# Entry of the second feed-forward block: two joins of squares by accumulating DMAs, two weights and tiles of the first operands sooner, differences in two steps

## The chip, the cores and the metric

The kernel runs on one core of one Trainium2 chip. The metric is the device time of one execution in microseconds (us); three runs of the kernel before took 2147.59, 2148.53 and 2149.14 us, median 2148.53. Five engines work side by side, each through its own queue in order: TensorE (PE, matmuls; PEld is its loading of weights), VectorE (DVE), ScalarE (ACT), GpSimd (POOL, here an issuer of DMAs) and SyncE (SP, an issuer of DMAs). They wait for each other through semaphores. ScalarE issues some DMAs too.

## What is computed

A decoder trunk of two layers on 1024 tokens with 1024 channels, in float32. Each layer is a mixer (a short gated convolution in the first, dilated attention in the second) and a SwiGLU feed-forward block of width 2816, each behind an RMS norm and with a residual sum:

```
def rms_norm(x, g):
    xf = x.astype(jnp.float32)
    y = xf * lax.rsqrt(jnp.mean(xf * xf, axis=-1, keepdims=True) + EPS)
    return (y * g.astype(jnp.float32)).astype(x.dtype)
...
def swiglu(h, w_gate, w_up, w_down):
    return (jax.nn.silu(h @ w_gate) * (h @ w_up)) @ w_down
...
    for i in range(DEPTH):
        h = rms_norm(x, mix_norm[i])
...
            x = x + dilated_attention_mixer(h, attn_w_qkv[j], attn_w_out[j], rel_bias)
        h = rms_norm(x, ffn_norm[i])
        x = x + swiglu(h, ffn_w_gate[i], ffn_w_up[i], ffn_w_down[i])
    return rms_norm(x, final_norm)
```

The place in question is the passage from the attention's output projection (`wo`) to the gate and up products of the second layer's feed-forward block: the residual x gets its last sums, its squares are summed over the channels, the reciprocal root is spread over all rows, and the scaled x becomes the operand of the next products.

## The kernel before

**Tiles.** The activations lie with channels on the 128 rows and tokens along them, as eight tiles `X[n]` of 128x1024. Nearly all work is done on halves of 512 tokens, one PSUM bank each. Every float32 operand is split in a high part (ScalarE, L139 for weights, L546 for activations) and a low part (VectorE, source minus high part, L140 and L547); one product then is three matmuls: high by high, high by low, low by high (L365 to L367 in `product`, L554 to L556 in `mm`).

**Strassen units.** Gate and up products are done by Strassen's seven products of 2x2 blocks. The blocks of the activations are the two halves of the channels (tiles 0 to 3, tiles 4 to 7) by the two halves of the tokens. Operand 1 is the first channels of the first token half, operand 2 the last channels of it; 6, 7, 4, 5 and 3 need the second token half or differences of the two. `unit_order` gives the order of (unit, product): n = 0 is (0, 1), then (1, 1), (0, 2), (1, 2), (2, 1), (2, 2), (3, 1), (3, 2), (0, 6), (1, 6), (0, 7), (1, 7), (0, 4), (1, 4), (0, 5), (1, 5) and so on. Each of these products is twelve matmuls of 128x512. `products` calls `start(n)` of `feed_forward` after the n-th one, and there the next preparations stand.

**Order of work.** The program is written out by hand in one order; every engine takes its instructions in that order. `ensure(upto)` has the weight splits made up to an index of the list `ops`, and `load_raw` with it the loads of raw weights that these need, through SP's queue.

**The output projection at the entry.** `by_columns` runs the last three of eight k tiles of `wo` over the first token half (j = 0), then over the second (j = 1), for n = 0 to 7. After each piece `add_to_x` sums the bank into x (L487), `added` has weights made, `each` is `Norm.chained` and squares the tile (L439), and `between` stores x to DRAM (the spill, L1286) and does the preparations of the feed-forward block. In the second pass, `between` first takes the statistics of the first token half: `Norm.stats` sums the squares over the rows with tiny matmuls (L466), takes root and reciprocal (L469, L470), makes diagonal tiles (L475), spreads them by a matmul (L482) and copies the result to `rstd` (L483). Then each step n does `step(k)`: one step of `first_half` (scale tile k of the first token half, L1107; high part L546; low part L547, one tile behind) and `gained(k)` (the second token half of tile k times its gain, L1129; from k = 4 on an accumulating DMA of POOL, L1133, makes tile k minus tile k-4 out of it).

**Sums of squares.** `chained` keeps two accumulators, `acc` for even and `odd` for odd tiles. Tiles 2 and 3 are added by accumulating DMAs of POOL (L442). From tile 4 on, in the second block (`late`), tile 4 is kept as `rest`; tiles 5 and 6 are added to it by VectorE (L454), `odd` is added to `acc` (L440) at tile 6, and at tile 7 `rest` and then the square of tile 7 are added to `acc`: five adds of VectorE. This goes for both token halves.

**The second half's operands.** After n = 2 (second block; 1 in the first) the statistics of the second token half begin, and after the next product `second_half` starts: its first stage makes operands 7 and 6; then, at n = 5, 7, 8, 10 and 12, one stage each: four differences for operand 4; its high and low parts with four multiplications by `rstd`; four differences for operand 5; parts of 5; parts of 3. VectorE does all but the high parts. The same `feed_forward` serves both blocks, with key 0 and 1.

Of the kernel before, what the change touches and what calls it, by code (L numbers as in the profile page):

```python
# [13 lines left out]
ALU = mybir.AluOpType  # L14
# [7 lines left out]
KT = D // 128  # L22
# [73 lines left out]
def trunk(ctx: ExitStack, tc: tile.TileContext, x, gains_in, cwi, ck, cwo, wqkv, wo, relb,  # L96
          wg, wu, wd, oneh, ident, out):
    nc = tc.nc
# [6 lines left out]
    def page(name, dt=F32):  # L105
        return pages.tile([128, 1024], dt, name=name, tag="page", bufs=PAGES)
# [3 lines left out]
    def half_page(name, dt=F32):  # L110
        return scope["pool"].tile([128, 512], dt, name=name, tag="half", bufs=scope["halves"])
# [4 lines left out]
    def half(h):  # L116
        return slice(h * HALF, (h + 1) * HALF)
# [42 lines left out]
    def ensure(upto):  # L160
        while op_state[0] < min(upto + 1, len(ops)):
            key = ops[op_state[0] + 1][0] if op_state[0] + 1 < len(ops) else None
            if key in sums_of:
                sums_of.pop(key)()
            made[op_state[0]] = ops[op_state[0]][1]()
            op_state[0] += 1
# [203 lines left out]
    def run(*gens):  # L370
        for _ in zip(*gens):
            pass
        for g in gens:
            for _ in g:
                pass
# [14 lines left out]
    class Norm:  # L390
# [30 lines left out]
        def add(self, k):  # L421

            hi, lo = page("h_hi", F32R), page("h_lo", F32R)
            nc.scalar.activation(hi, X[k], AF.Identity, scale=self.gain(k))
            nc.vector.scalar_tensor_tensor(lo, X[k], self.gain(k), hi, op0=ALU.mult, op1=ALU.subtract)
            self.h[k] = (hi, lo)
            self.square(k)

        def chained(self, k, c0, c1, late):


            s = slice(c0, c1)
            if self.acc is None:
                self.acc, self.rstd = page("acc"), page("rstd")
            acc = self.acc[:, s]
            if k == 1:
                self.odd = half_page("acc2")
            to = half_page("sq") if k > 1 else self.odd if k else acc
            nc.scalar.activation(to, X[k][:, s], AF.Square)  # L439
            add = lambda t: nc.vector.tensor_tensor(out=acc, in0=acc, in1=t, op=ALU.add)  # L440
            if k in (2, 3):
                nc.gpsimd.dma_start(out=(acc, self.odd)[k % 2], in_=to, accum_op=ALU.add)  # L442
            if k > 3:
                self.flush()
                self.put_off = lambda: add(to)
            if k == KT - 2:
                add(self.odd)
                self.odd = None
            if not late or k < 4:
                return  # L450
            if k == 4:
                self.rest, self.put_off = to, None
            elif k < KT - 1:
                add = lambda t: nc.vector.tensor_tensor(out=self.rest, in0=self.rest, in1=t, op=ALU.add)  # L454
            else:
                add(self.rest)
                self.rest = None
# [27 lines left out]
    def add_to_x(n, banks):  # L485
        for (c0, c1), b in banks.items():
            nc.vector.tensor_tensor(out=X[n][:, c0:c1], in0=X[n][:, c0:c1], in1=b[:, :c1 - c0], op=ALU.add)  # L487
# [608 lines left out]
    class Swiglu(Strassen):  # L1096
# [38 lines left out]
        def second_half(self):  # L1135

            tt = lambda out, a, b, op: nc.vector.tensor_tensor(out=out, in0=a, in1=b, op=op)
            rstd = self.norm.rstd[:, half(1)]
            t3, h, f = self.xd, {k: self.xg[4 + k] for k in range(4)}, self.f
            t2 = {k: X[4 + k][:, half(1)] for k in range(4)}  # L1140
            low7, low = [], None
            for k in range(4):
                tt(t3[k], t3[k], rstd, ALU.mult)
                low7.append(self.hi(7, k, t3[k]))
            for k in range(4):
                tt(t2[k], t3[k], f[k], ALU.add)
                nxt = self.hi(6, k, t2[k])
                if low:
                    low()
                low = nxt  # L1150
            low7.pop(0)()
            low()
            for lo in low7:
                lo()
            yield

            for k in range(4):
                tt(f[4 + k], f[4 + k], t2[k], ALU.subtract)
            yield
            lows = [self.hi(4, k, f[4 + k]) for k in range(4)]  # L1160
            for k in range(4):
                tt(h[k], h[k], rstd, ALU.mult)
            for lo in lows:
                lo()
            yield
            for k in range(4):
                tt(f[k], h[k], t2[k], ALU.subtract)
            yield
            lows = [self.hi(5, k, f[k]) for k in range(4)]
            for lo in lows:  # L1170
                lo()
            yield
            lows = [self.hi(3, k, h[k]) for k in range(4)]
            for lo in lows:
                lo()
            X[:] = [None] * KT
# [31 lines left out]
        def feed_forward(self, stats, last_step, after, final=None):  # L1208
            prep = []

            def start(n):
                if n == 0:
                    last_step()
                    for m in (6, 7):
                        combos[self.key, 1](m)
                    ensure(self.at(3, 1))
                if n == self.key + 1:
                    next(stats)
                    combos[self.key, 2](6)
                    ensure(self.at(0, 6))  # L1220
                elif n == self.key + 2:
                    run(stats)
                    prep.append(self.second_half())
                    next(prep[0])
                    nc.scalar.activation(scratch, eps, AF.Silu)
                    ensure(self.at(1, 6))
                elif n == 4:
                    ensure(self.at(1, 7))
                elif n in (5, 7, 8, 10, 12):
                    next(prep[0], None)  # L1230
                if n in (8, 24):
                    self.ahead = 3 if n == 8 else 2

            self.run(start)
            key = ("d", self.key)
            if final:
                final(key, self.plain, self.hid)
                return
            for n in range(KT):
                add_to_x(n, both(take(key + (n,)), self.plain, self.hid))  # L1240
                after(n)
# [22 lines left out]
    def into_ffn(i, norm):  # L1264

        sw = Swiglu(i, norm)

        pre = []
        first_op = [k for k, f in ops].index(("m", (i, 0), 1))

        def step(k):
            next(pre[0], None)
            sw.gained(k)

        def group1(key, ks, acts):
            def added(j, n):

                if j == 0 and n > 2:
                    if 3 < n < KT - 2:
                        ensure(op_state[1] + 1)  # L1280
                    ensure(first_op + n - 2)
                elif j and n in (2, 3):
                    ensure(first_op + n + 4)

            def between(j, n):
                nc.scalar.dma_start(spill[n][:, half(j)], X[n][:, half(j)])  # L1286
                if j == 0:
                    if n == 2:
                        load_raw(raw_base[i] + 3)
                    elif n == 3:  # L1290
                        if not i:
                            nc.scalar.activation(less, gains, AF.Copy, scale=-1.0)
                    elif n == 4 and last_part:
                        last_part.pop()()
                    elif n == KT - 1:
                        norm.flush()
                    return
                if n == i:
                    pre.append(norm.stats(0, HALF))
                    next(pre[0])  # L1300
                    for m in (6, 7):
                        combos[i, 0](m)
                elif n == i + 1:
                    run(pre.pop())
                    pre.append(sw.first_half())
                for k in (((), (0,), (1,), (2, 3), (4,)), ((), (), (0, 1), (2, 3), (4,)))[i][n] if n < 5 else (n,):
                    step(k)

            by_columns((key, 1), ks, acts, HALVES, lambda n, c: norm.chained(n, *c, i), between,
                       AO_WIDE if key == "ao" else 4, added=added)  # L1310

        def last_step():
            run(pre[0])
            norm.flush()

        return sw, group1, norm.stats(HALF, S), last_step
# [620 lines left out]
```

## Time and profile before

| | |
|---|---|
| runs, median (lowest to highest) | 2148.53 us (2147.59 to 2149.14) |
| profiled execution, its own time | 2150.36 us |
| its span, first to last instruction | 2148.5 us |
| mean granted TensorE clock | 0.996 |
| half clock, second entry | 1508.0 to 1514.8 us |
| second pass of the output projection | about 1480 to 1497 us |
| first gate and up products of the second block | from 1496.8 us |

How to read the lines that follow: a timeline row gives start, duration, engine, line, operation, output and input tiles, shape and count, and in brackets the idle time ahead of it with what ended it. A row of a chain gives start, duration, what. A row of a list of waits gives the engine and its line, what released it, the sum of the waits, how many, the longest. A row of a stretch gives the busy time and count of PE, PEld, DVE, ACT and POOL, then the granted clock, the DMA engines' mean busy share and GB/s. A row of DMA issues ends with the size of one and the median time from issue to landing in us; a queue's row has packets, MB and the share of sixteen DMA engines' time. Durations of instructions that follow each other on one engine overlap by some 0.1 us, so a start-to-start distance is shorter than a duration (0.60 for 0.69 on VectorE). Line numbers are those of the kernel before.

### The profile page before, as it was taken

The numbers are of one execution on the slowest core, as the hardware profiler recorded it, in microseconds if no ns is written. First come the engines' busy times: TensorE is split into PE (matmuls) and PEld (weight loads), VectorE is DVE, ScalarE is ACT, GpSimd is POOL, SyncE is SP. The second block draws the span as 40 slices with busy tenths as digits, with TensorE's granted clock in tenths as the row PEclk, the third lists the DMA queues.
The fourth block names the chain that finished last, engine by engine and source line by source line (L and its number), as shares of the span: only waits on it lengthen the run. The fifth ranks groups of instructions, "written<-read, shape, count | busy, mean of one in ns | idle before, by whom it ended". The sixth has DMA issues, their size and how long they took to land.

```text
span 2148.5 us, 30610 instructions
## 1 busy us (share of the span) xinstructions
PE 2122.4 (99%) x11158; PEld 1819.3 (85%) x11158; DVE 1721.4 (80%) x3192; ACT 1011.3 (47%) x1836; POOL 183.6 (9%) x239
## 2 busy tenths in 40 slices
PE   9999999999999999999999999999999999999998
PEld 7788888888888888878999999888788888888887
DVE  7898769988888888865777777777998888888886
ACT  7433426443444564344555555535544444456435
POOL 1000000110101000010111111111010101001000
PEclk9999999999999999999999999999999999999999
DMA  7222642223332576323333333636223332368432
GB/s 227 84 94 69 225 132 74 103 99 108 113 109 98 171 220 194 113 63 128 89 93 93 93 93 86 193 120 188 64 80 107 113 108 103 102 206 231 163 94 79
DMA packets 135055, 264.49 MB, mean 123 GB/s; under 512 B 47912, under 2 KB 59192, under 8 KB 134906
## 3 DMA queue, kind: packets, MB, share of 16 engines
q1 hardware_dynamic: 74106, 177.99, 26.0%
q0 software_dynamic: 19632, 61.46, 9.2%
q10 hardware_dynamic: 41168, 23.10, 3.5%
q8 instruction: 88, 1.44, 0.3%
q14 instruction: 61, 0.50, 0.1%
HBM read 188.88 MB, written 66.27 MB: 119 GB/s over the span
## 4 chain that ended last, share of the span: by engine, by line
PE 88%; DVE 6%; ACT 3%; issue 2%; DMA 1%; SPq 0%; ACTq 0%; DVEq 0%
PE bank L554 18%; PE bank L556 18%; PE bank L555 17%; PE bank L367 6%; PE bank L365 6%; PE bank L366 6%; PE bank L1529 5%; PE bank L646 3%; PE bank L649 3%; PE bank L648 3%; PE bank L1457 1%; PE bank L1456 1%; DVE w L140 1%; PE bank L1397 1%; PE bank L1396 1%
## 5 line engine op out<-in xcount | busy, mean ns | idle before, releaser
L554 PE MATMUL bank<-b,w 128*128 128x512 f32 x1784 | 698.7, 392 | 3.6 <-ACT part L560 2.1
L556 PE MATMUL bank<-b,w 128*128 128x512 f32 x1784 | 696.5, 390 | 4.4 <-DVE w L140 4.4
L555 PE MATMUL bank<-b,w 128*128 128x512 f32 x1784 | 696.8, 391 | 2.8 <-DVE b L547 2.2
L556 PEld LDWEIGHTS bank<-b,w 128*128 128x128 f32 x1784 | 335.8, 188 | 77.3 <-DVE w L140 7.3
L554 PEld LDWEIGHTS bank<-b,w 128*128 128x128 f32 x1784 | 335.9, 188 | 74.5 <-ACT part L560 3.3
L555 PEld LDWEIGHTS bank<-b,w 128*128 128x128 f32 x1784 | 336.1, 188 | 72.9 <-DVE b L547 3.1
L139 ACT ACTIVATE w<-combo 128x512 fp32r<-128x512 f32 (+2 forms) x464 | 233.9, 536 | 223.0 <-DVE combo L187 188.1
L140 DVE TENSOR_TENSOR w<-combo,w 128x512 fp32r<-128x512 f32 (+2 forms) x464 | 260.4, 575 | 39.0 <-ACT w L139 38.3
L560 ACT ACTIVATE part<-bank 128x512 f32<-128x512 f32 x168 | 100.2, 597 | 375.5 <-PE bank L556 373.9
L140 DVE TENSOR_TENSOR w<-raw,w 128x512 fp32r<-128x512 f32 (+2 forms) x316 | 170.5, 560 | 36.7 <-ACT w L139 36.7
L564 DVE TENSOR_TENSOR part<-part,bank 128x256 f32<-128x256 f32 (+1 forms) x348 | 158.7, 488 | 26.9 <-PE bank L556 16.2
L139 ACT ACTIVATE w<-raw 128x512 fp32r<-128x512 f32 (+2 forms) x316 | 150.5, 520 | 45.9 <-DVE w L140 11.2
L365 PE MATMUL bank<-w_hi,w 128*128 128x512 f32 (+1 forms) x320 | 119.7, 374 | 1.0 <-ACT w L139 1.0
L367 PE MATMUL bank<-w_hi,w 128*128 128x512 f32 (+1 forms) x320 | 118.0, 369 | 0.7 <-DVE w L140 0.7
L366 PE MATMUL bank<-w_lo,w 128*128 128x512 f32 (+1 forms) x320 | 117.8, 368 | 0.0
L784 DVE TENSOR_TENSOR x<-x,bank 128x512 f32<-128x512 f32 x136 | 92.8, 682 | 29.3 <-PE bank L556 29.3
L487 DVE TENSOR_TENSOR x<-x,bank 128x512 f32<-128x512 f32 (+1 forms) x104 | 66.1, 643 | 54.5 <-PE bank L367 52.7
L365 PE MATMUL bank<-h_hi,w_hi 128*128 128x512 f32 x256 | 104.5, 408 | 0.2 <-ACT w_hi L139 0.2
L187 DVE TENSOR_TENSOR combo<-raw 128x512 f32<-128x512 f32 (+1 forms) x160 | 103.2, 645 | 0.0
L367 PE MATMUL bank<-h_hi,w_lo 128*128 128x512 f32 x256 | 100.2, 391 | 0.6 <-DVE w_lo L140 0.5
L366 PE MATMUL bank<-h_lo,w_hi 128*128 128x512 f32 x256 | 99.9, 390 | 0.0
L1552 ACT ACTIVATE z<-bank 64x512 f32<-64x512 f32 x32 | 19.0, 594 | 145.3 <-PE bank L1529 145.3
(261 smaller groups left out, 3889.8 us busy)
## 6 DMA issues: line engine op xcount, KB each, us to landing
hin<-part SPq DMA_DIRECT2D x126, 256.0 KB
raw<-in_ffn_w_gate SPq DMA_DIRECT2D x44, 512.0 KB
raw<-in_ffn_w_up SPq DMA_DIRECT2D x44, 512.0 KB
part<-sum POOLq DMA_DIRECT2D x72, 256.0 KB, 2.3
raw<-in_ffn_w_down SPq DMA_DIRECT2D x48, 384.0 KB
raw<-in_conv_w_in SPq DMA_DIRECT2D x24, 512.0 KB
raw<-in_attn_w_qkv SPq DMA_DIRECT2D x24, 512.0 KB
part<-part POOLq DMA_DIRECT2D x36, 256.0 KB, 2.4
```

Source lines behind the costliest of these rows:

```text
L139: nc.scalar.activation(hi, src, AF.Copy)
L140: eng.tensor_tensor(out=lo, in0=src, in1=hi, op=ALU.subtract)
L187: eng.tensor_tensor(out=c, in0=a, in1=b, op=op)
L365: nc.tensor.matmul(b, whi[:, a], ahi[:, s], start=first, stop=False)
L366: nc.tensor.matmul(b, whi[:, a], alo[:, s], start=False, stop=False)
L367: nc.tensor.matmul(b, wlo[:, a], ahi[:, s], start=False, stop=last)
L554: nc.tensor.matmul(b, hi[:, a], bhi, start=start and k == 0, stop=False, skip_group_check=True)
L555: nc.tensor.matmul(b, hi[:, a], blo, start=False, stop=False, skip_group_check=True)
L556: nc.tensor.matmul(b, lo[:, a], bhi, start=False, stop=k == n - 1, skip_group_check=True)
L560: nc.scalar.activation(t, b, AF.Copy)
L564: nc.vector.tensor_tensor(out=t, in0=t, in1=b, op=ALU.add)
L1529: nc.tensor.matmul(view(acc[ih], off, dims), vx[:, u, 64 * a:64 * a + 128], rhs, start=first, stop=last)
```

## The change

Four edits, in `chained`, `second_half` with `feed_forward`, `added`, and `between`:

- In the second block and the second token half alone, `odd` goes into `acc` by an accumulating DMA at tile 4, and the square of tile 5 into `rest` by another at tile 5. Tile 6 is added to `acc` by VectorE, as are `rest` and tile 7: three adds.
- The four differences for operand 4 are two stages of two, and n = 9 takes a stage too. So the stages stand at n = 5, 7, 8, 9, 10 and 12: two differences, two differences, parts of 4 with the multiplications, differences for 5, parts of 5, parts of 3 (both blocks).
- In the second block the weights of products (3, 1) and (3, 2) are split at n = 1 and 2 of the second pass, before at n = 2 and 3.
- In the second block `first_half` takes two steps at each of n = 2, 3 and 4 and one at each of n = 5, 6 and 7, apart from `gained`; before it took one with each `gained`, two at n = 2 and 3, one at n = 4 to 7, and the last low part behind the loop.

```
@@ chained
+            if late and c0:
+                if k == 4:
+                    self.rest = to
+                    nc.gpsimd.dma_start(out=acc, in_=self.odd, accum_op=ALU.add)
+                    self.odd = None
+                elif k == 5:
+                    nc.gpsimd.dma_start(out=self.rest, in_=to, accum_op=ALU.add)
+                elif k > 5:
+                    self.flush()
+                    self.put_off = lambda: add(to)
+                if k == KT - 1:
+                    add(self.rest)
+                    self.rest = None
+                return
@@ second_half
             for k in range(4):
                 tt(f[4 + k], f[4 + k], t2[k], ALU.subtract)
-            yield
+                if k % 2:
+                    yield
@@ feed_forward
-                elif n in (5, 7, 8, 10, 12):
+                elif n in (5, 7, 8, 9, 10, 12):
                     next(prep[0], None)
@@ added
-                elif j and n in (2, 3):
-                    ensure(first_op + n + 4)
+                elif j and n in (2 - i, 3 - i):
+                    ensure(first_op + n + 4 + i)
@@ between
-                for k in (((), (0,), (1,), (2, 3), (4,)), ((), (), (0, 1), (2, 3), (4,)))[i][n] if n < 5 else (n,):
-                    step(k)
+                if i:
+                    for _ in range((0, 0, 2, 2, 2, 1, 1, 1)[n]):
+                        next(pre[0], None)
+                    for k in ((), (), (0, 1), (2, 3))[n] if n < 4 else (n,):
+                        sw.gained(k)
+                else:
+                    for k in ((), (0,), (1,), (2, 3))[n] if n < 4 else (n,):
+                        step(k)
```

In the changed order of the engines, PE's instructions and SP's are the same; VectorE has two adds fewer, ScalarE the same instructions in another order, POOL two DMAs more. POOL's queue in the second token half is: square 2 into `acc`, square 3 into `odd`, `odd` into `acc` (which waits for both to land), the first difference, square 5 into `rest`, the other three differences. On VectorE the add of square 6 waits for the third of these, the add of `rest` for the fifth, and the low part of the last tile of operand 2 stands behind both.

## The prediction

> **What bounds the kernel now.** I read the page first, then the list of PE's waits, then the stretch of the second entry in stretches, by engine and along the chain.
>
> ```profile
> span 2148.5 us, 30610 instructions
> PE 2122.4 (99%) x11158; PEld 1819.3 (85%) x11158; DVE 1721.4 (80%) x3192; ACT 1011.3 (47%) x1836; POOL 183.6 (9%) x239
> PE 88%; DVE 6%; ACT 3%; issue 2%; DMA 1%; SPq 0%; ACTq 0%; DVEq 0%
> ```
>
> TensorE is the bound: it idles 26 us in all. The change takes no matmul away, so it can only win PE's stalls at this entry, and lose by new ones.
>
> ```profile
> PE bank L555 <- DVE b L547: 2.2, 1, 2.2
> PE bank L556 <- DVE w L140: 1.0, 1, 1.0
> ...
> 1500.00:1505.00 5.00, 3.96 (x18) 2.88 (x16) 4.96 (x9) 2.92 (x5) 1.68 (x2) 1.00 0.88 219
> ...
> 1510.00:1515.00 5.00, 5.00 (x12) 3.65 (x12) 2.38 (x4) 0.07 (x1) 0.00 (x0) 0.52 0.00 0
> 1515.00:1520.00 5.00, 5.00 (x22) 3.95 (x21) 3.70 (x6) 3.59 (x6) 0.00 (x0) 1.00 0.00 0
> ```
>
> Two waits stand between 1440 and 1560 us, both for VectorE, which is full there (4.96 of 5 us). At full speed 22 matmuls take 5 us, 0.227 each. Right behind the first wait only 12 fit into 5 us, at a granted clock of 0.52: the stall is paid twice.
>
> ```profile
> 1503.57 0.39 PE L554 MATMUL bank<-b,w 128*128 128x512 f32 x1
> 1506.20 0.50 PE L555 MATMUL bank<-b,w 128*128 128x512 f32 x1 [2.24 <-DVE b L547]
> ...
> 1507.65 1.60 PE L466 MATMUL bank<-ones,acc 128*128 128x1 f32 x8
> ...
> 1538.89 0.50 PE L556 MATMUL bank<-b,w 128*128 128x512 f32 x1 [0.99 <-DVE w L140]
> ...
> 952.16 0.50 PE L365 MATMUL bank<-w_hi,w 128*128 128x512 f32 x1 [1.04 <-ACT w L139]
> ```
>
> ```profile
> 344.91 1.05 PE bank L466 x8
> 348.86 0.86 PE bank L482 x2
> ...
> 1507.78 1.47 PE bank L466 x8
> 1514.58 1.04 PE bank L482 x2
> ```
>
> From 1503.57 to 1507.65 PE starts six matmuls; at 0.227 they need 1.36 of the 4.08 us, so 2.72 are lost. The same statistics, twelve matmuls and spreading take 349.72 - 344.91 = 4.81 us in the first block and 1515.62 - 1507.78 = 7.84 here: 3.03 more, the half clock. The first stall costs 5.75. The second costs its 0.99 and 0.11 of a slow first matmul (0.50 for 0.39): 1.1.
>
> [...]
>
> **The change part by part.** *First operands and joins.* In VectorE's queue of the second half, before:
>
> ```profile
> 1489.22 1.42 DVE L1107 SCALAR_TENSOR_TENSOR hcol<-x,gains,rstd 128x512 f32<-128x512 f32 x2 [0.58 <-ACT rstd L483]
> 1492.94 0.69 DVE L140 TENSOR_TENSOR w<-raw,w 128x512 fp32r<-128x512 f32 x1 [0.98 <-ACT w L139]
> 1500.40 0.68 DVE L454 TENSOR_TENSOR sq<-sq 128x512 f32<-128x512 f32 x1
> 1503.47 0.68 DVE L454 TENSOR_TENSOR sq<-sq 128x512 f32<-128x512 f32 x1
> 1506.30 0.69 DVE L547 TENSOR_TENSOR b<-hcol,b 128x512 fp32r<-128x512 f32 x1 [0.15 <-ACT b L546]
> ```
>
> The last low part, which PE needs, starts at 1506.30. The change takes two of five square adds out (0.60 each, start to start; 0.69 when alone), moves a weight's low part (0.60, and its 0.98 of waiting) ahead of the first scaling, and prepares tiles 5 to 7 one step sooner. I walk the new queue from the first scaling (0.57 later, below): eight scalings at 0.66, eight low parts at 0.60 and five residual adds at 0.60, with 0.4 of waits for ScalarE, bring it to the two square adds at 1502.7 and 1503.4, the last low part at 1504.0 to 1504.7, the last square at 1504.7 to 1505.4. PE without its stall would want the last low part four matmuls after 1503.57, at 1504.48, and, 0.57 later like the rest, at 1505.05; two matmuls on, at 1505.52, it wants the sum. It is met, with 0.1 to 0.3 us to spare, if neither add waits for its DMA; both stand ahead of the last low part, and everything behind them waits too.
>
> ```profile
> 1493.73 0.85 POOL L442 DMA_DIRECT2D acc<-sq  x1 [3.89 <-ACT sq L439]
> ...
> acc<-sq POOLq DMA_DIRECT2D x8, 256.0 KB, 3.6
> ...
> q8 instruction: 1, 0.02, 33.4%
> ...
> acc<-sq POOLq DMA_DIRECT2D x1, 256.0 KB, 6.1
> ...
> q0 software_dynamic: 225, 0.40, 55.1%
> ```
>
> No row shows a DMA that waits for another here, so its price is bounded. The odd square's transfer (1493.73 before) starts by the same walk 0.24 later, at 1493.97. With the median 3.6 it lands at 1497.6; the join issues at 1497.75 and lands by 1501.4, ahead of 1502.7. Behind it POOL issues the first difference at 1499.25 (ScalarE has scaled its tile by 1498.95) and, 0.85 later, the second join at 1500.1; with 3.6 and 0.1 behind a spill it lands at 1503.8, and the add starts at 1503.85 for 1503.4. The last square add, which wants the sum before it, ends near 1505.8, and PE's statistics start at 1505.85: 0.33 lost. From below nothing is lost. From above the odd transfer takes 6.1, as in this very profile, where a block of instructions was fetched just then (the q8 row, the half microsecond from 1493.5) and a weight load began: then it lands at 1500.07, the join goes out at 1500.2 and lands near 1503.7, and the second join is two transfers behind it. A transfer takes 1.4 us of all engines (55.1% of 4 us for 0.40 MB is 2.2; for 0.26 MB 1.4), so it lands at 1506.5, with a spill between near 1506.9, and the statistics, 1.95 behind it (three adds and the low part), start at 1508.85: 3.33 lost. I take 0.33: 3.6 is the median of eight, 6.1 one case.
>
> [...]
>
> *The first weight sooner.* ScalarE now splits it between the squares of tiles 0 and 1.
>
> ```profile
> 1483.65 0.63 ACT L439 ACTIVATE acc<-x 128x512 f32<-128x512 f32 x1
> 1484.31 0.26 ACT L469 ACTIVATE r<-bank,eps 128x4 f32<-128x4 f32 x1
> 1484.82 0.69 DVE L475 TENSOR_TENSOR diag<-eye,r 128x512 f32<-128x512 f32 x1
> 1485.57 1.12 PE L482 MATMUL bank<-diag,ones 128*128 128x512 f32 x2
> ```
>
> The root, the diagonal and PE's spreading follow each other without slack (diagonal done 1485.51, PE 1485.57); one more activation ahead of the root, 0.57 start to start, stalls PE by as much. Below: nothing, if PE had slack; above: 0.7. I take 0.57; the stall is shorter than the 1.04 at 952 us, at full clock.
>
> *A load that moves with it.* The sixth block's weight load changes its semaphore lane: in SP's queue it now waits for a spill of the first half to land, in place of an earlier load.
>
> ```profile
> q1 hardware_dynamic: 74106, 177.99, 26.0%
> ...
> 1460.95 5.54 SPq L153 DMA_DIRECT2D raw<-in_ffn_w_up  x2
> 1472.81 1.82 POOL L442 DMA_DIRECT2D acc<-sq  x2 [3.39 <-DMA spill<-x]
> 1478.41 0.69 DVE L440 TENSOR_TENSOR acc<-acc,acc 128x512 f32<-128x512 f32 x1
> 1482.52 1.01 PE L466 MATMUL bank<-ones,acc 128*128 128x1 f32 x8
> ```
>
> So it goes from the end of the 1460.95 row (1466.5) to about the time at which POOL, too, was let go by spills: among the two accumulating transfers of 1472.81, which VectorE takes at 1478.41; from there to PE's 1482.52 its queue is full, so a late landing stalls PE by as much. The second of the two, issued near 1473.7, lands by the median at 1477.3, 1.1 to spare. Queue 1 spent 26.0% of 2148.5 us on 177.99 MB, 1.6 us for the 0.52 MB of one load. PE loses 0 if the load stays behind, up to 1.6 if it goes ahead and its first packets are slow; I take 0.6, near the 0.5 by which 1.6 exceeds 1.1. SP's next load waits for PE anyway.
>
> *Differences in two steps.* Four stages of the second half move by one product in both blocks.
>
> ```profile
> 1530.33 2.49 DVE L1137 TENSOR_TENSOR x<-x,rstd 128x512 f32<-128x512 f32 x4
> 1535.14 0.68 DVE L564 TENSOR_TENSOR part<-part,bank 128x512 f32<-128x512 f32 x1
> 1535.74 2.49 DVE L1137 TENSOR_TENSOR hcol<-x 128x512 f32<-128x512 f32 x4
> 1538.15 1.29 DVE L140 TENSOR_TENSOR w<-raw,w 128x512 fp32r<-128x512 f32 x2
> ```
>
> The weight's low part that PE waits for at 1538.89 comes ahead of the four differences of 1535.74, at 1535.74 itself, 2.4 sooner than 1538.15; the wait of 1.1 goes. The add of 1535.14 goes ahead of the four multiplies; the four low parts behind it come 0.6 later and are wanted two products on, so they cost nothing; without that cover 0.6. In the first block the same stages have no wait to remove: 0, at most 0.6.
>
> Sum against the profiled execution (2150.36, its span 2148.5): -5.75 - 1.1 + 0.33 + 0.57 + 0.6 = -5.35, so 2145.0. The runs' median, 2148.53, is 1.83 below that execution; I take the same sum off it: 2143.2.
>
> **The rivals.** *The joins land late (slower).* The odd transfer again takes 6.1: 3.33 in place of 0.33, and a gap of over 3 us in PE brings the half clock back (3.03): -5.35 + 3.0 + 3.03 = +0.7, 2149.2; with the clock low for as long again (3.03) and the upper bounds (1.7) 2153.9. For it: the load and PE's fetch keep their places to PE's work. Against: 3.6 is usual, no other landing shown is near 6.1. It decides from a landing of about 5.4 us.
>
> *Halfway.* At 4.6 the second join lands near 1505.1 and PE loses 1.5, between the 1.04 that kept the clock and the 2.24 that did not: 2144.4 without the half clock, 2147.4 with it.
>
> *The half clock is this execution's own.* If the timed runs go on at full speed behind the stall, 3.03 can't be won: 2146.2. For it: the profiled execution is slower than all three runs. Against: 1.83 is less than 3.03. [...]
>
> **How the numbers follow.** Forecast 0.53, late joins 0.22, half clock absent 0.14, halfway 0.11. About 0.2% (4.3 us) tells a change from none here. Of the forecast 0.47 lies below 2144.2, of halfway 0.03: faster 0.50. Of the late joins 0.10 lies above 2152.8: slower 0.10. The rest, 0.40, is no change that can be told. The forecast's own range is 2141.7 (none of the three new prices paid) to 2144.9 (1.6 for the load, 0.7 for the weight, 0.6 in the first block); the range reaches from 2141.5 to 2150.5, which leaves out the worse half of the late joins and a little below.
>
> **What would show it.** Right: no PE wait for L547's low parts near 1505, granted clock 1.00 from 1500 to 1520, no wait for the weight at 1538, and a new PE stall near 0.6 at the first spreading. The joins: landings of 3 to 4 us in POOL's issues, VectorE's two square adds back to back. Wrong: VectorE idle until a DMA ahead of the last low part, a clock of 0.5 behind it, or a wait of the first statistics for squares that land after 1478.

## The result and the profile after

| | before | after |
|---|---|---|
| median (lowest to highest), 21 runs each | 2148.96 (2145.55 to 2150.90) | 2153.47 us (2150.16 to 2156.24) |
| profiled execution, its span | 2150.36, 2148.5 | 2150.39, 2148.4 us |
| ratio of the runs | | 1.002, 95% interval 1.0015 to 1.0026 |

The change costs 4.5 us where 5.3 were forecast to be won. The profiled execution shows little of it: among the runs of each kernel it is one of the slowest of before and the second fastest of after. The list of PE's waits of after between 1440 and 1560 us (line numbers behind the new block of `chained` are 14 higher here than before; a row has PE's line, what released it, the sum, how many, the longest):

```profile
PE bank L480 <- DVE acc L440: 2.9, 1, 2.9
PE bank L569 <- DVE b L561: 1.1, 1, 1.1
PE bank L568 <- DVE part L578: 0.5, 1, 0.5
PE bank L568 <- ACT part L574: 0.4, 1, 0.4
```

The two waits of before (2.2 for the last low part, 1.0 for a weight) have become 1.1 and nothing. A wait of 2.9 is new, ahead of the statistics of the first token half, where before had none, and two of 0.5 and 0.4 for `part` come behind the differences. In the timeline of after:

```profile
1459.71 12.66 SPq L153 DMA_DIRECT2D raw<-in_ffn_w_up  x2
...
1480.28 0.69 DVE L440 TENSOR_TENSOR acc<-acc,acc 128x512 f32<-128x512 f32 x1 [3.03 <-DMA acc<-sq]
...
1484.35 1.87 PE L480 MATMUL bank<-ones,acc 128*128 128x1 f32 x8 [2.91 <-DVE acc L440]
...
1496.31 0.85 POOL L442 DMA_DIRECT2D acc<-sq  x1 [3.52 <-ACT sq L439]
1497.43 0.33 SPq L153 DMA_DIRECT2D raw<-in_ffn_w_gate  x1
1500.39 0.84 POOL L446 DMA_DIRECT2D acc<-acc  x1 [3.23 <-DMA acc<-sq]
1502.14 1.12 POOL L449 DMA_DIRECT2D sq<-sq  x1
...
1508.89 0.69 DVE L440 TENSOR_TENSOR acc<-acc,sq 128x512 f32<-128x512 f32 x1 [3.22 <-DMA sq<-sq]
...
1510.24 0.50 PE L569 MATMUL bank<-b,w 128*128 128x512 f32 x1 [1.06 <-DVE b L561]
...
1535.74 0.69 DVE L140 TENSOR_TENSOR w<-raw,w 128x512 fp32r<-128x512 f32 x1
```

Three things are to be seen. The sixth block's load, the second of the first row, leaves SP's queue at 1472 (1459.71 + 12.66) in place of 1466.5, among the accumulating transfers of the first token half; VectorE then waits 3.03 for these. The second join (`sq<-sq`) lands 6.7 us after its issue, and VectorE waits 3.22 for it with the last low part behind. The weight's low part of 1535.74 comes ahead of the differences, as the forecast said. The granted clock, by stretches of 3.41 us (the third figure from the end of a row):

```profile
1480.32:1483.73 3.41, 1.12 (x5) 0.58 (x4) 3.27 (x6) 0.63 (x1) 0.00 (x0) 0.98 0.21 79
1483.73:1487.14 3.41, 2.79 (x11) 2.60 (x12) 2.64 (x6) 2.19 (x5) 0.00 (x0) 0.50 0.40 154
1487.14:1490.56 3.42, 3.42 (x9) 2.58 (x8) 2.84 (x5) 0.27 (x1) 0.00 (x0) 0.52 0.00 0
```

The half clock has moved with the stall, from 1508 to 1484, and lasts two stretches as before. So two suspects stand out, the load that moved and the joins, and the profile alone does not say which of them the runs pay for.

### The profile page after: what moved, and what is told of

Read it like the earlier page. It is cut to its first block, busy times and chain, and to the rows that moved or that the text cites. A ratio compares the mean times of both kernels' runs of the same rounds, so it can differ in the third digit from the quotient of the medians.

```text
span 2148.4 us, 30615 instructions
## 1 busy us (share of the span) xinstructions
PE 2121.5 (99%) x11158; PEld 1819.5 (85%) x11158; DVE 1720.5 (80%) x3190; ACT 1012.1 (47%) x1836; POOL 185.4 (9%) x241
```

## The experiments

Theory L: the moved load is the loss. Theory J: the joins land late, and usual runs pay more for it than this profile shows. All times are medians of 10 or 11 runs; the ratios, with their 95% intervals, are to runs of the kernel before beside them (32 or 33 for every four kernels, with medians of 2148.58, 2148.59 and 2148.76 us). The ratios come from all runs, so they need not be the quotient of the two medians. An interval is about 0.0009 to either side, 1.9 us, so differences of less than 2 us between kernels are not settled by the times alone. Kernels that are compared with each other did not all run side by side; the kernel before came out at 2148.58 to 2148.96 each time. Line numbers differ by up to 15 in the rows shown of these kernels; names of tiles and operations do not.

**The load put back.** The load is asked for at the end of the first pass; in SP's queue it then waits for an earlier load again. All four edits stay.

```
                     elif n == KT - 1:
-                        norm.flush()
+                        norm.flush(), i and load_raw(raw_base[i] + 5)
```

> All four edits stay; the sixth block's weight load is asked for at the end of the first pass, so that in SP's queue it waits again for an earlier load and not for a spill. Theory L (the moved load makes the squares of the first token half land late; PE's stall of 2.9 ahead of the first statistics and the half clock behind it, 3, are its price): both vanish, 5 to 6 us below the changed kernel, 1 to 2 us below the kernel before (ratio 0.9993 to 0.9997). Theory J (the accumulating joins of the second half land late and are what the timed runs pay): the wait of the first statistics vanishes in the trace too, but the time stays 2 to 4 us above the kernel before (ratio 1.001 to 1.002), as the DMA wait of VectorE near 1505 stays and brings the half clock there.

Measured: 2151.64 us, 1.0017 (1.0008 to 1.0025). Waits, timeline and chain of this kernel:

```profile
PE bank L569 <- DVE b L561: 4.3, 1, 4.3
```

```profile
1459.12 5.15 SPq L153 DMA_DIRECT2D raw<-in_ffn_w_up  x2
1491.48 0.33 SPq L153 DMA_DIRECT2D raw<-in_ffn_w_gate  x1
```

```profile
1491.94 6.90 DMA acc<-sq
1498.89 0.49 issue
1500.47 5.62 DMA sq<-sq
```

The wait of the first statistics is gone, and yet the kernel is slower than before: theory J, at the values that it gave. The chain (start, duration, what; "issue" is time in which the engine waited for nothing that the profile shows) has the joins in a row: the odd square's transfer takes 6.9, the first join goes out only then, the second behind it takes 5.6, and PE waits 4.3 for the low part behind the add. The clock is at half from 1506.0 to 1516.2, three stretches. What is left for the load are the 1.8 us between 2153.47 and 2151.64, which the times alone do not settle.

**One edit, and all but one.** The weights alone on the kernel before (the load moves with them), and the changed kernel without its joins (the new block of `chained` left out):

```
-                elif j and n in (2, 3):
-                    ensure(first_op + n + 4)
+                elif j and n in (2 - i, 3 - i):
+                    ensure(first_op + n + 4 + i)
```

> The kernel before with only the two weights sooner; the load moves with them. Theory L: the wait of the first statistics (2 to 3 us) and a half clock (3) come on top of the kernel before, 5 to 7 us above it (ratio 1.0023 to 1.0033). Theory J: within 1 us of it (at most the 0.6 of the split on ScalarE ahead of the root), ratio 1.0000 to 1.0005.

> The changed kernel with the five adds of VectorE in place of the two joins; the other three edits stay, the moved load too. Theory L: the wait of the first statistics stays, the time stays 2 to 5 us above the kernel before (1.001 to 1.0023). Theory J: VectorE no longer waits for a DMA near 1505, the stall there is at most 1.5 us and brings no half clock; 0 to 3 us below the kernel before (0.9986 to 1.0000).

Measured: the weights alone 2148.62, 1.0002 (0.9994 to 1.0011); without joins 2147.80, 0.9999 (0.999 to 1.0008). PE's waits in each, the weights alone first:

```profile
PE bank L555 <- DVE b L547: 2.2, 1, 2.2
PE bank L466 <- DVE acc L440: 2.2, 1, 2.2
```

```profile
PE bank L466 <- DVE acc L440: 3.2, 1, 3.2
```

The load moves in both (it leaves SP's queue at 1472.4 and 1472.1), and PE waits 2.2 and 3.2 ahead of the first statistics in both. Theory L was right about the wait and wrong about the 4.5 us: without the joins these are gone.

**Tiles and steps alone**, neither joins nor weights:

> The kernel before with tiles 5 to 7 of the first operand one step sooner and the differences in two steps; no joins, weights where they were, so the load does not move. Theory L and theory J give the same here: no wait of the first statistics, no DMA wait of VectorE; the first stall shrinks from 2.7 to between 0.7 and 1.4 us without the half clock and the weight's wait (1.1) is gone: 3 to 6 us below the kernel before (0.9972 to 0.9986). If neither theory holds and the new order of the tiles itself costs time, it is not below.

Measured: 2148.82, 1.0004 (0.9995 to 1.0012), a miss for both theories. Its profile shows the stall ahead of the last low part down to 0.7, but a wait of 2.8 ahead of the first statistics although the load stands where it stood before: VectorE waited for the last load of the attention's z, which stands in its queue ahead of the adds of the first token half's squares, and the first accumulating transfers landed in 5.6 and 6.2 us (3.8 and 4.4 before):

```profile
1476.50 0.69 DVE L1591 TENSOR_TENSOR o<-o,z 128x512 f32<-128x512 f32 x1 [3.06 <-DMA z<-rdram]
```

So this wait can come without the moved load. Over the fourteen profiles of this study it stands in all four with the load moved (2.2 to 3.2) and, of the ten with the load kept, in just the three in which VectorE waited for z (this one, and 1.1 and 2.3 further down). The profiled execution (2151.35) is the slowest of the eleven, so it does not explain their median. Why these two edits win nothing by themselves, while beside the weights and with the load kept they win 3.5 us (2147.89 to 2144.38, both below), stays open.

**The joins alone** on the kernel before:

```
+            if late and c0:
+                if k == 4:
...
+                    nc.gpsimd.dma_start(out=acc, in_=self.odd, accum_op=ALU.add)
...
+                elif k == 5:
+                    nc.gpsimd.dma_start(out=self.rest, in_=to, accum_op=ALU.add)
```

> The kernel before with the two joins alone. Theory J: the odd square lands 6 to 7 us after its issue as in four of the five profiles so far that show it beside a weight load (6.1, 7.7, 6.6, 6.1, 6.9; 3.5 once), so the joins go out near 1500 and 1501 and the second lands near 1507; the last low part, which stands behind the adds, starts near 1508 in place of 1506.3: 1 to 2 us more stall and up to one more window of half clock (1.7): 1 to 4 us above the kernel before (1.0005 to 1.0019). The rival, that the joins cost only beside the other edits: 0 to 1.2 us below it (two adds of VectorE less).

Measured: 2152.67, 1.002 (1.0011 to 1.0029). The joins by themselves cost 4.1 us, the upper end of theory J. (The landings listed ahead of this run are those of six profiles, five of them late.) Waits:

```profile
PE bank L569 <- DVE b L561: 4.6, 1, 4.6
```

2.2 has become 4.6: two adds taken off the engine that set the end made it later.

**What makes the odd square late.** With the load put back, the next block's load goes out through POOL's queue, behind the last difference:

```
-            nc.sync.dma_start(raw_tile[i][:, :raw_src[i].shape[1]], raw_src[i])
+            (nc.gpsimd if 1 in raw_base and i == raw_base[1] + 6 else nc.sync).dma_start(raw_tile[i][:, :raw_src[i].shape[1]], raw_src[i])
```

> The four edits with the sixth block's load put back (as in the first experiment), and the seventh block's load, which went out on SP's queue within a microsecond of the odd square's transfer, goes through POOL's queue behind the last difference. Theory R (this load is what makes the odd square late): the odd square lands in 4.2 us or less, the joins land before VectorE's adds, the stall ahead of the last low part is 1.1 us or less and brings no half clock: 2144 to 2148. Theory F (a block of instructions fetched at that time, 0.9 to 2.7 us long, is what makes it late): 6 us or more as before, 2151 to 2152, as with the load put back alone.

Measured: 2148.22, 1.0002 (0.9993 to 1.0011). The timeline:

```profile
1491.91 0.84 POOL L442 DMA_DIRECT2D acc<-sq  x1 [3.51 <-ACT sq L439]
1496.75 0.83 POOL L446 DMA_DIRECT2D acc<-acc  x1 [4.00 <-DMA acc<-sq]
1497.84 1.47 POOL L449 DMA_DIRECT2D sq<-sq  x1
1503.78 0.69 DVE L440 TENSOR_TENSOR acc<-acc,sq 128x512 f32<-128x512 f32 x1 [2.67 <-DMA sq<-sq]
```

The odd square lands in 4.3 in place of 6.9, and 3.4 us come back: theory R, mostly. A block of instructions was fetched here too while the odd square was on its way (the queue's row between 1492 and 1496 us: packets, MB, share):

```profile
q8 instruction: 1, 0.02, 2.1%
```

In all fourteen profiles such a fetch falls between the issue and the landing of the odd square, for 0.9 to 3.3 us of one DMA engine (the row's share, times the time, times 16), beside landings of 3.4 as beside 7.7 (1.3 us beside 4.3 here, 1.7 beside 3.5 in the first profile of after, 2.6 beside 6.1 in before), so theory F falls. But the load is not all: the second join, queued behind the first and a difference, still takes 5.8 and VectorE still waits 2.67, with a stall of 1.9 in PE. The landing of the odd square in all fourteen profiles, against the issue of that load relative to its own, and what the load's queue moved until that landing:

| load issued, relative to the transfer | landing of the odd square, us | queue 1 meanwhile, MB |
|---|---|---|
| 0.85 to 0.33 us ahead (eight profiles, before among them) | 6.1, 5.2, 6.2, 6.4, 6.9, 5.8, 6.7, 7.7 | 0.52 in each |
| 0.57 to 0.66 us behind (three) | 6.6, 6.2, 6.1 | 0.52 in each |
| 1.12 us behind (the first profile of after) | 3.5 | 0.12 |
| 1.46 us behind (one) | 3.4 | 0.08 |
| gone from there (this experiment) | 4.3 | none |

In the eleven late landings the whole load, 0.52 MB, moved while the odd square was on its way; in the three others little or nothing of it did.

**The best version: no joins, load put back.** Tiles, weights and steps as changed, with the first experiment's line and without the new block of `chained`:

> Tiles, weights and steps as changed, no joins, and the sixth block's load put back. Theory L (the moved load costs PE 2 to 3 us ahead of the first statistics, and 0 to 2 windows of half clock): that wait is gone, 2 to 4 us below the run without joins (2147.8): 2144 to 2146, ratio 0.998 to 0.999. If the moved load is hidden without the joins: 2147 to 2148.

Measured: 2144.38, 0.9981 (0.9972 to 0.999): the fastest kernel of all here, 4.2 us below before. The granted clock falls nowhere in this execution but at its end; its mean is 0.999, the highest of the fourteen profiles. Its waits:

```profile
PE bank L466 <- DVE acc L440: 1.1, 1, 1.1
PE bank L555 <- DVE b L547: 0.5, 1, 0.5
PE bank L554 <- DVE part L564: 0.4, 1, 0.4
PE bank L554 <- ACT part L560: 0.4, 1, 0.4
PE bank L482 <- DVE diag L475: 0.3, 1, 0.3
```

The load is worth 3.4 us here (2147.80 to 2144.38), as theory L said, and the joins 7.3 (2151.64 to 2144.38): in the two profiles, a stall of 4.3 with three stretches of half clock against one of 0.5 with none. With the seventh block's load out of the odd square's way the joins still cost 3.8 (2148.22). The 1.1 ahead of the first statistics is late z again: VectorE waited 1.35 for it.

**The second join alone.** As in the first experiment, but `odd` is added by VectorE at tile 6, as before:

```
                 if k == 4:
                     self.rest = to
-                    nc.gpsimd.dma_start(out=acc, in_=self.odd, accum_op=ALU.add)
-                    self.odd = None
...
+                if k == KT - 2:
+                    add(self.odd)
+                    self.odd = None
```

> As with the load put back, but the odd accumulator is added by VectorE at tile 6 as before and only the square of tile 5 goes by an accumulating DMA, which is then not behind a join that waits for the odd square. Theory J with the odd square as its root: the second join goes out near 1499 and lands by 1504, VectorE waits less than 1 us for it: 2145 to 2148. If any accumulating DMA so late costs the same: 2150 to 2152.

Measured: 2145.00 (2144.15 to 2151.10), 0.999 (0.9981 to 0.9999). The second join now goes out at 1499.39, 1.08 sooner than behind the first one, lands in 4.8, and VectorE waits 0.88 for it:

```profile
1504.24 0.69 DVE L440 TENSOR_TENSOR acc<-acc,sq 128x512 f32<-128x512 f32 x1 [0.88 <-DMA sq<-sq]
```

So nearly all the price (6.6 of 7.3 us, 2151.64 to 2145.00) hangs on the first join, which waits for the odd square and holds POOL's queue meanwhile (6.59 us idle ahead of it with the load put back). The second one alone wins nothing that shows either (2145.00 against 2144.38).

**The other three edits, one at a time.** The weights alone with the load kept; then the best version with the differences in one step; then with the tiles in the order of before:

> The kernel before with only the two weights sooner, the sixth block's load kept where it was. Theory L: the weights alone with the load moved came out level with the kernel before although PE waited 2.2 us more, so without that wait they are 2 to 3.4 us below it: 2145.2 to 2146.6 (0.9984 to 0.9990). The rival, that the weights are worth nothing and the moved load costs nothing in the timed runs of this kernel: 2148 to 2149 (0.9998 to 1.0003).

> Tiles and weights as changed, load put back, no joins, and the differences in one step as before. The forecast put two steps at 1.1 us, the wait for the weight's low part; the profiles of the kernels with two steps show that wait gone, but two new ones of 0.5 and 0.4 us behind the adds and copies of part. If these are its price, two steps are worth 0.2 us: 2144.4 to 2144.9. By the forecast's 1.1: 2145.5.

> Weights and steps as changed, load put back, no joins, and the tiles of the first operand in the order of the kernel before. The stall ahead of the last low part goes from 0.5 back towards 2.2 us, and with it come one or two windows of half clock (1.7 each): 2146.5 to 2149.5. If the tiles' order is worth nothing without the joins: 2144 to 2145.

Measured: 2147.89, 0.9997 (0.9988 to 1.0006); 2145.65, 0.9986 (0.9977 to 0.9995); 2146.84, 0.9994 (0.9985 to 1.0003). The first is nearer the rival: the weights alone are worth nothing that shows. Its profile had a wait of 2.3 ahead of the first statistics with the load kept, and VectorE waiting 2.49 for z. The tiles are worth 2.5 us; the 1.3 of the step is within the error. Waits of the last two, in that order:

```profile
PE bank L556 <- DVE w L140: 1.0, 1, 1.0
...
```

```profile
PE bank L555 <- DVE b L547: 1.3, 1, 1.3
...
```

With one step the weight's wait is back and the two waits for `part` are gone: 1.0 against the 0.8 of the best version.

**The changed kernel once more**, for a second profile:

> The changed kernel as it is, for a second profile. If its first profile, whose odd square landed in 3.5 us, was the exception that its place among the runs suggests (the second lowest of 21), a usual one shows the odd square landing in 6 us or more, VectorE waiting for both joins, and a stall ahead of the last low part of 3 us or more on top of the 2 to 3 us ahead of the first statistics: 2152 to 2154. If 3.5 is usual here because the moved load delays what follows, the stall is 1.1 again, and the 4.5 us that the runs lie above the kernel before need another cause.

Measured: 2153.60, 1.0022 (1.0013 to 1.0032). Waits and timeline:

```profile
PE bank L569 <- DVE b L561: 2.9, 1, 2.9
PE bank L480 <- DVE acc L440: 2.2, 1, 2.2
```

```profile
1494.17 0.84 POOL L442 DMA_DIRECT2D acc<-sq  x1 [3.52 <-ACT sq L439]
1494.79 0.33 SPq L153 DMA_DIRECT2D raw<-in_ffn_w_gate  x1
1500.93 0.83 POOL L446 DMA_DIRECT2D acc<-acc  x1 [5.92 <-DMA acc<-sq]
1502.03 1.47 POOL L449 DMA_DIRECT2D sq<-sq  x1
1504.50 0.69 DVE L440 TENSOR_TENSOR acc<-acc,sq 128x512 f32<-128x512 f32 x1 [1.74 <-DMA acc<-acc]
1508.11 0.69 DVE L440 TENSOR_TENSOR acc<-acc,sq 128x512 f32<-128x512 f32 x1 [2.91 <-DMA sq<-sq]
```

This execution (2152.39) is nearer to the runs' median than the first one (2150.39). It has both stalls, both followed by half clock (0.52 from 1485.3, 0.50 and 0.52 from 1509.2), and VectorE waits for one join and then for the other. In the first profile the load happened to go out 1.12 us behind the odd square.

## Why the prediction was wrong

Set against 10.3 us between 2143.2 and 2153.47:

| term of the sum | forecast | measured | from |
|---|---|---|---|
| joins | +0.33 | +7.3 | load put back, with and without joins |
| load that moves | +0.6 | +1.8 (3.4 without joins) | with all four edits, load moved and put back |
| tiles, steps and weight (-5.75 - 1.1 + 0.57) | -6.3 | -4.2 | best version against 2148.59 |

The three errors, 7.0, 1.2 and 2.1, add up to 10.3 because the rows are steps on one path from the kernel before to the changed one. On another path, with the load moved first, the joins cost 5.7 (2147.80 to 2153.47) and the load 3.4; by themselves the joins cost 4.1.

- **Joins: the step that failed** is "I take 0.33: 3.6 is the median of eight, 6.1 one case." The 6.1 was the landing of this very transfer in this very place; the eight were the same line at eight places of two entries, and 3.6 says nothing of this one. Eleven of fourteen profiles gave 5.2 to 7.7. The rival "the joins land late" had the mechanism, and 2153.47 lies inside its 2149.2 to 2153.9; its point of decision, a landing of 5.4, was passed in all of the eleven but one. The forecast gave it a chance of 0.22 because of a median over unlike places. The 0.33 also holds no half clock; with the load put back the joins brought a stall of 4.3 and three stretches of it. That "no other landing shown is near 6.1" was an argument from rows that could not bear on it.
- **The second join** was given 3.6 and 0.1 for a spill; 5.6 to 6.7 were measured in the five profiles that have both. Two more transfers of POOL stand directly ahead of it, and it lands late even where the odd square does not (first profile of after: 3.5, then 6.7).
- **The load that moves** was seen, and its path to PE too, but its bound of 1.6 (one load's engine time) was too low: the transfers of the first token half landed in 6.2 to 8.2 us in the four profiles with the load moved, against 3.7 to 5.0 in the seven with it kept and z in time (5.1 to 7.1 in the three with late z). PE waited 2.2 to 3.2. The term also lacked the half clock that followed the stall in three of these four profiles (two stretches behind 2.9 us, one behind 3.2 and one behind 2.2; none behind the other 2.2), although the other stall had been charged for it.
- **Tiles sooner** did what was said of them, smaller: 1.3 to 0.5 in the wait ahead of the last low part, 2.5 us in the times, both without the joins. The walk of VectorE's queue speaks of eight low parts ahead of the two adds, but its 1502.7 comes out with seven; the eighth stands behind them. It left 0.1 to 0.3 us to spare without any wait for a join, where the best version, with no joins, shows a stall of 0.5.
- **The first stall's 5.75** held 3.03 of half clock from one execution. The rival "the half clock is this execution's own" was partly right: the best version wins 4.2, with a profile free of half clock but at its end (mean 0.999). The runs of before spread with the clock: of 98, the 31 with a mean granted clock of 0.998 took 2146.8 us in the mean, the 49 with 0.997 took 2148.7, the 17 with 0.996 took 2150.5 (one more, at 0.999, took 2145.4). One stretch of 3.41 us at half clock costs an estimated 1.7 us (half of 3.41) and 0.0008 of mean clock (1.7 of 2148), and the rows go by 1.8 to 1.9 us for 0.001. This fits a number of such stretches that differs from run to run, where the forecast had one fixed price. Some lie outside this entry: eight of the fourteen profiles have one near 26 or near 944 us (the first of after from 944.4 to 947.8, the tiles and steps alone from 27.8 and from 946.0). The profile of before has one from 26.6 to 30.0, which at 1.7 us would be nearly all of the 1.83 by which it lay above the runs' median.
- **The first weight sooner** was put at 0.57 ahead of the spreading; 0.3 was measured where PE is at full clock, inside its bounds.
- **Two steps**: the weight's wait went as forecast, and 0.8 to 0.9 came back as waits for `part`, the add and the copies that were put ahead of the differences. That the four low parts come 0.6 later and "cost nothing" held, as PE waits for none of them; what was overlooked is the work for the banks. Whether anything is left of the 1.1 is open (1.3 by the times, within their error).

Not settled: why z lands late in some executions (three of the fourteen profiles). That the runs of after differ from its first profile by the place of the load alone was seen in two profiles, not counted over all runs.

## What to carry to other kernels

Price a DMA by the rows of its own place and neighbours, not by the median of its line: here one landing took 3.4 to 4.3 us without a load that moved its bytes meanwhile and 5.2 to 7.7 with it, and a second transfer queued behind one that waits for this landing was late with it (5.6 to 6.7). Here an add of 0.6 us on a full engine was cheaper than an accumulating DMA for which the same engine then waited 2.7 to 3.2 us, as the low part that PE needed next stood behind that wait. When weights are split sooner, look at which transfer each load now waits for, and ask for the load explicitly where it used to go out.

## What the runs showed of the hardware

At the places named here the half clock came in whole stretches of 3.41 us (to within 0.2): one from 944.4 in the first profile of after, two from 1483.7 in it, three from 1506.0 with the load put back. In the second profile of the changed kernel, cut on that grid (1485.32 and 1509.21 are seven stretches apart):

```profile
1478.49:1481.90 3.41, 2.20 (x10) 1.50 (x8) 3.08 (x5) 0.63 (x1) 0.00 (x0) 1.00 0.34 131
1481.90:1485.32 3.42, 2.46 (x15) 2.15 (x16) 2.69 (x5) 1.86 (x5) 0.00 (x0) 0.98 0.31 122
1485.32:1488.73 3.41, 3.41 (x8) 1.93 (x7) 3.23 (x6) 0.60 (x2) 0.00 (x0) 0.52 0.08 32
1488.73:1492.14 3.41, 3.41 (x17) 2.77 (x16) 2.79 (x6) 2.39 (x5) 0.83 (x1) 1.00 0.50 133
...
1505.80:1509.21 3.41, 0.75 (x4) 0.29 (x2) 1.10 (x2) 0.00 (x0) 0.31 (x1) 0.98 1.13 214
1509.21:1512.62 3.41, 3.17 (x12) 2.87 (x13) 2.80 (x6) 0.41 (x2) 0.00 (x0) 0.50 0.66 119
1512.62:1516.04 3.42, 3.42 (x10) 2.71 (x9) 2.65 (x5) 0.37 (x1) 0.00 (x0) 0.52 0.00 0
```

The stall of 2.17 us straddles an edge of the grid, leaves PE busy for 2.20 and 2.46, and costs one stretch; that of 2.9 lies nearly whole inside one, leaves 0.75, and costs two; the 4.3 with the load put back cost three. With the weights alone a stall as long as the first cost none, here ahead of the first statistics, on that execution's own grid:

```profile
1479.74:1483.16 3.42, 1.53 (x7) 0.94 (x5) 3.28 (x6) 0.63 (x1) 0.00 (x0) 1.00 0.21 80
1483.16:1486.57 3.41, 3.13 (x17) 2.51 (x17) 2.64 (x6) 2.46 (x5) 0.00 (x0) 1.00 0.40 154
1486.57:1489.98 3.41, 3.11 (x12) 2.18 (x12) 3.38 (x6) 0.50 (x1) 0.00 (x0) 1.00 0.00 0
```

So the price of a stall near 2.2 us went from nothing to two stretches (3.4 us, the profile of before). The grid lies elsewhere in each of these executions: the edges at 1483.73 and 1485.32, in the two profiles of the changed kernel, are 0.47 of a stretch apart. Where a stall falls on it is one suspect, but the rows give no rule: the clock fell behind two successive stretches with 2.20 and 2.46 us of busy PE, 4.66 in sum, and stayed up behind 1.53 and 3.13 with the weights alone, 4.66 too. It even fell without a wait of PE: from 944.4 us in the first profile of after, behind a stretch in which PE's row is full, 3.41 of 3.41, but 2.59 us of it are eight matmuls of L519 with weights of 33*16 in place of 128*128. What decides was not tried.

The landing of an accumulating transfer of 256 KB of squares went from 3.1 us (tile 2 of the second token half, in all fourteen profiles) to 8.2 us (first token half, without joins) at this entry, 5.1 us apart for the same size.
